# The last gathered tile's value rows are summed on VectorE, and VectorE makes all splits of the dense products

## The chip, the cores and the metric

The kernel runs on one core of one Trainium2 chip. The metric is the device time of one execution in microseconds: before the change the median of three runs is 3572.51 us (3567.39 to 3578.01).

## The reference

One encoder layer on 1024 tokens of width 1024, in float32. The change lies in its last part, PEER, a choice of single-neuron experts. Per block of 128 tokens:

```python
s = einsum('thpd,hpkd->thpk', (xb @ w_q)..., sub_keys)      # 8 heads, 2 halves, 128 keys
idx, best_s = 16 best of the sums of the two halves' 16 best  # per head: 128 experts a token
gate = softmax(best_s)
h = gelu(einsum('thkd,td->thk', u_table[idx], xb), approximate=False)
return einsum('thk,thkd->td', gate * h, v_table[idx])
```

The tables u and v have 16384 rows of 1024 numbers. The result is added to alpha times the block's input, and a LayerNorm gives the output.

## The kernel before

The tokens are eight tiles of 128. The front (projections, attention, the recurrent branch, merge, first LayerNorm) is not touched; each tile's input of PEER is left in HBM as x1d. PEER is done in two ways.

**Gathered tiles** (GATHERED = 0, 1, 2, 6, 7). For each of a tile's 128 choices GpSimd gathers 128 rows of u (one a token) into a place of a ring, 128x1024 float32 or 0.524 MB (experts_in, line 1461), and VectorE multiplies the place with the tile and sums along it (line 1467). After Gelu and the gate the 128x128 coefficients go to HBM. Later the class Rows reads them, turns them with TensorE, gathers rows of v (line 1763) and lets TensorE sum them: a step takes two places, and issues four matmuls, in the profile 8 records named pg, with the coefficients in a sliding window (win). A tile has 64 steps; its sums go through HBM (yd) and finals adds them to alpha times x1d, normalizes and stores, tile after tile.

**Dense tiles** (DENSE = 3, 4, 5). All 16384 experts are evaluated, and the selection is a sparse coefficient matrix. A loop over j = 0 to 127 takes 128 columns of U and rows of V each turn: hidden(j+1, m) makes 24 matmuls of 384 columns into the one PSUM buffer b; csplit(j+1) applies Gelu on ScalarE and multiplies with the selections on VectorE (line 1648), which frees b; values(j, m) makes 18 matmuls of 512 columns (v). Every float32 operand is split in two float32r halves, high by a ScalarE copy (line 291) and low by a subtraction (line 292). usplit and vsplit make four such splits of 128x512 a turn: of U the first on VectorE and the second on GpSimd (UPOOL = (0, 1)), of V every second one on GpSimd (VPAT). The coefficients' split cl is VectorE's. U and V columns come on SP's queue, two and three buffers deep; the coefficients of j >= 44 are reloaded from HBM four at a time.

**The order** is fixed when the program is made. Two background queues put their work between the matmuls: each mm call gives them credit by an estimated duration (columns / 2400 us; line 274 is in mm), times a rate. g.B holds top-k and experts_in of all gathered tiles, whose step k costs 1.46; g.V holds the value steps of Rows, 3 each, two by two in the loop. In the loop the rates are RATEB[1] = 0.46 and RATEV[1] = 0.52, and RATEV[2] = 1.25 once the last gathered tile's u part is done. Each turn also advances finals twice. Instructions of one engine run in this order; GpSimd's queue holds the gathers of both streams and the splits.

After the loop finals adds the dense sums in PSUM to alpha times x1d, normalizes the three tiles and stores them.

Of the kernel before, what the change touches and what calls it, by code (L numbers as in the profile page):

```python
# [10 lines left out]
F32 = mybir.dt.float32  # L11
# [4 lines left out]
AF = mybir.ActivationFunctionType  # L16
OP = mybir.AluOpType
# [9 lines left out]
TKI = 1  # L27
RATEP = (1, 1, 0.9)

RATEB = (2.1, 0.46)  # L30
RATEV = (4.2, 0.52, 1.25)
SEL = (1, 2, 3)
DENSE = (3, 4, 5)
GATHERED = (0, 1, 2, 6, 7)
LATE = (4, 5, 6)

RING = 7
# [3 lines left out]
VCOST = 3.0  # L41
XAT = 14
AENG = "XY"
UPOOL = (0, 1)
VPAT = (0, 2, 4, 6)
VBUF = 3
UBUF = 2
LOMOD = 8
# [13 lines left out]
ALPHA = 2.0 ** 0.25  # L62
# [210 lines left out]
def mm(g, o, l, r, start, stop_):  # L273
    g.pe.matmul(o, l, r, start=start, stop=stop_)  # L274
    n = 1
    for d in r.shape[1:]:
        n *= d
    us = max(n, 256) / 2400.0 if r.dtype == F32R else max(4 * n, 256) / 2400.0
    g.V.tick(us)
    if not g.V.busy:  # L280
        g.B.tick(us)


def mm3(g, o, lh, ll, rh, rl, start, stop_):
    mm(g, o, lh, rh, start, False)
    mm(g, o, lh, rl, False, False)
    mm(g, o, ll, rh, False, stop_)


def split(g, hi, lo, src, lo_eng=None):  # L290
    g.act.copy(hi, src)  # L291
    (lo_eng or g.dve).tensor_sub(lo, src, hi.bitcast(F32))  # L292


class Weights:
# [58 lines left out]
    def ahead(self, most=1):  # L354
        while self.ns <= min(self.n + most * (self.n > 3), self.first - 1):
            self._split()
        while self.ns == self.first and self.nl < len(self.order) and self.nl <= self.n + most:
            self._fetch()
# [21 lines left out]
def run(gen):  # L380
    for _ in gen:
        pass
# [19 lines left out]
def body(ctx, g):  # L402
# [101 lines left out]
    g.spare, g.over = True, False  # L504
    g.rows = Rows(g, GATHERED)
    g.rows.places.add([g.vx.tile([128, D], F32, name=f"vr{i}") for i in range(RING)])
# [754 lines left out]
def layer_norm(g, mt, z):  # L1261

    dve, act = g.dve, g.act
    st = mt.tile([128, 2, 6], F32, name="st", bufs=3)
    for i in range(2):
        dve.bn_stats(st[:, i, :], z[:, i * 512:(i + 1) * 512])
    yield
    mv = mt.tile([128, 2], F32, name="mv", bufs=3)
    dve.bn_aggr(mv, st)
    rs = mt.tile([128, 1], F32, name="rs", bufs=3)  # L1270
    act.activation(rs, mv[:, 1:2], AF.Sqrt, bias=g.eps[:, 1:2])
    yield
    dve.reciprocal(rs, rs)
    yield

    def scale(z, gb):
        dve.scalar_tensor_tensor(z, z, mv[:, 0:1], gb[0], op0=OP.subtract, op1=OP.mult)  # L1277
        dve.scalar_tensor_tensor(z, z, rs, gb[1], op0=OP.mult, op1=OP.add)  # L1278

    yield scale  # L1280
# [166 lines left out]
def experts_in(g, tile_):  # L1447

    dve, act, pool, sp, A, P = g.dve, g.act, g.pool, g.sp, g.A, g.gp
    idx = P.tile([128, 128], I32, name="eidx", bufs=1)  # L1450
    sp.dma_start(idx, g.seld[tile_])
    xt = P.tile([128, D], F32, name="ext")
    sp.dma_start(xt, g.x1d[tile_])
    hh = P.tile([128, 128], F32, name="hh", bufs=1)
    keys, n = g.keys, 0
    yield 1.0
    yield 1.0
    for k in range(128):
        while n < 128 and len(keys.free) > 1:
            keys.alive[n] = place = keys.take()  # L1460
            pool.indirect_dma_start(out=place, out_offset=None, in_=A["u"], in_offset=bass.IndirectOffsetOnAxis(ap=idx[:, n:n + 1], axis=0))  # L1461
            n += 1
        if k == 0:
            yield 1.0
            yield 1.0
        gg = keys.alive.pop(k)
        dve.tensor_tensor_reduce(out=gg, in0=gg, in1=xt, scale=1.0, scalar=0.0, op0=OP.mult, op1=OP.add, accum_out=hh[:, k:k + 1])  # L1467
        keys.give(gg)
        yield 1.46
    if "hh" in g.dbg:  # L1470
        sp.dma_start(g.dbg["hh"][tile_ * 128:(tile_ + 1) * 128, :], hh)
    gate = idx.bitcast(F32)
    sp.dma_start(gate, g.gated[tile_])
    act.activation(hh, hh, AF.Gelu)
    dve.tensor_mul(hh, hh, gate)
    act.dma_start(g.cijd[tile_][:, 0, :], hh)
    yield 0.1


def parts(C, i, a, b):  # L1480

    return [C[:, i, j:j + 8, :].rearrange("p j t -> p (j t)") for j in range(a, b - 7, 8)]


def dense_block(g, C):


    tc, nc, A, ident = g.tc, g.nc, g.A, g.ident
    dve, act, pool, sp, pe = g.dve, g.act, g.pool, g.sp, g.pe
    tiles = DENSE  # L1490
    nt = len(tiles)
    n = nt * 128
# [53 lines left out]

    g.B.rate, g.V.rate = RATEB[0], RATEV[0]
    zx = ExitStack()
# [6 lines left out]
    with tc.tile_pool(name="bp", bufs=BLEAD + 1) as bp, tc.tile_pool(name="cj", bufs=2) as cj:  # L1555
        ab, pb = {}, {}
        for k in range(-BLEAD - 4, n4 + 1):
# [23 lines left out]
            if k > 0:  # L1581
                e = k - 1
                i, o = 4 * e // BLK, 4 * e % BLK
# [7 lines left out]
        run(xt)  # L1591
    g.B.rate, g.V.rate = RATEB[1], RATEV[1]
    u_hl, v_hl, c_hl, phs = {}, {}, {}, {}
    po = [[g.psV.tile([128, 512], F32, name=f"v{i}{m}") for m in range(2)] for i in range(nt)]
# [30 lines left out]
    def usplit(q):  # L1625
        if q < 256:
            u_hl[q] = [lp.tile([128, 512], F32R, name=f"u{x}") for x in "hl"]
            o = q % 2 * 512
            split(g, *u_hl[q], us[q // 2][:, o:o + 512], pool if UPOOL[q % 2] else dve)
            if o:  # L1630
                uload(q // 2 + UBUF)

    def vsplit(q):
        if q < 256:
            v_hl[q] = [lp.tile([128, 512], F32R, name=f"v{x}") for x in "hl"]
            o = q % 2 * 512
            split(g, *v_hl[q], raws[q // 2][:, o:o + 512], pool if q % 8 in VPAT else dve)
            if o:
                load(q // 2 + VBUF)
# [25 lines left out]

    def values(j, m):
        ch, cl = c_hl[j]
        vh, vl = v_hl.pop(2 * j + m)
        for i in range(nt):
            s = slice(i * 128, (i + 1) * 128)  # L1670
            mm3(g, po[i][m], ch[:, s], cl[:, s], vh, vl, j == 0, j == 127)
        if m:
            c_hl.pop(j)

# [12 lines left out]
    fin, old = iter(()), [p for j in range(LOOP, HALF - 7, 8) for i in range(nt) for p in parts(C, i, j, j + 8)]  # L1687
    g.rows.pairs = True
    for j in range(128):
        hidden(j + 1, 0)  # L1690
        usplit(2 * j + 4)
        hidden(j + 1, 1)
        usplit(2 * j + 5)
        csplit(j + 1)
        values(j, 0)
        vsplit(2 * j + 2)
        next(fin, None)
        values(j, 1)
        vsplit(2 * j + 3)
        next(fin, None)  # L1700
        if f"g{GATHERED[-1]}" in g.B.done:
            g.V.rate = RATEV[2]
        if j == 126:

            act.activation(cT[:, 0, 0:1], g.eps[:, 1:2], AF.Sqrt)

        k = (j + 1 - LOOP) // 8 * nt
        if (j + 1) % 8 == 0 and 0 < k <= len(old):
            (g.keys if k == nt else g.rows.places).add(old[k - nt:min(k, len(old) - 4)])
        if j == HALF:  # L1710
            fin = finals(g, tiles, po, old[-4:] + old[0:nt])
    assert f"v{GATHERED[-1]}" in g.V.done
    g.over = True
    run(fin)
    lx.close()
# [101 lines left out]
def finals(g, tiles, po, places):  # L1817


    A, dve, act, sp = g.A, g.dve, g.act, g.sp  # L1820
    gb = places[0:2]
    for m in range(2):
        sp.dma_start(gb[m], A["ln"][2 + m:3 + m, :].to_broadcast([128, D]))
    zd = places[4:7]

    def add(z, y):
        for m in range(2):
            zm = z[:, m * 512:(m + 1) * 512]
            dve.scalar_tensor_tensor(zm, zm, ALPHA, y[m], op0=OP.mult, op1=OP.add)

    z, y = places[2:4]
    for t in GATHERED:
        sp.dma_start(z, g.x1d[t])
        if t == GATHERED[-1]:
            while f"g{t}" not in g.B.done:
                yield
            for t_, z_ in zip(tiles, zd):
                sp.dma_start(z_, g.x1d[t_])
        while f"v{t}" not in g.V.done:
            yield  # L1840
        for _ in range(2):
            yield
        sp.dma_start(y, g.yd[t])
        for _ in range(3):
            yield
        add(z, [y[:, 0:512], y[:, 512:1024]])
        yield
        ln = layer_norm(g, g.pp, z)
        for _ in range(3):
            next(ln)  # L1850
            yield
        next(ln)(z, gb)
        yield
        sp.dma_start(A["out"][t * 128:(t + 1) * 128, :], z)
        yield
    while not g.over:
        yield
    lns = []
    for i, z in enumerate(zd):
        add(z, po[i])  # L1860
        lns.append(layer_norm(g, g.pp, z))
    for _ in range(3):
        for ln in lns:
            next(ln)
    for t, z, ln in zip(tiles, zd, lns):
        next(ln)(z, gb)
        sp.dma_start(A["out"][t * 128:(t + 1) * 128, :], z)


def _pack_w(w):  # L1870
# [54 lines left out]
```

## Time and profile before

| | us |
|---|---|
| median of 3 runs | 3572.51 |
| the profiled execution | 3567.98 |
| its span | 3566.2 |
| PE busy | 3168.3 |
| VectorE (DVE) busy | 2252.5 |
| GpSimd (POOL) busy | 2051.0 |
| ScalarE (ACT) busy | 1161.9 |

The dense loop fills about 2195 to 3543 us of the span. The profile gives busy time by engine and by stretch, groups of equal instructions with their mean duration, what ended each wait, and the chain of work that ended last. A matmul's record overlaps the next one, so the time of a run of matmuls is taken from start to start or from the chain. DMA share is the mean busy share of the 16 DMA engines; packets in flight together can take it a little over 1.

### The profile page before, as it was taken

Reading aid. Unit: us, or ns where it says so; the run is one execution under the profiler, and the core shown is the slowest. Engines: PE = TensorE matmul, PEld = TensorE weight load, DVE = VectorE, ACT = ScalarE, POOL = GpSimd, SP = SyncE. Lnnn points to the kernel's source line nnn. Section 1 sums busy time; section 2 is a strip of 40 time slices with the busy share of each in tenths; the row PEclk is TensorE's granted clock in tenths of the full one; section 3 lists DMA queues with packets and bytes.
Section 4 is the critical chain, followed back from the end, with each engine's and each line's share of the span. In section 5 each row is a group of like instructions: output and inputs, shape, how many; then the busy total and the mean of one; then the engine's idle time right before and its main releaser. Section 6 shows DMA issues by size and latency. Waiting matters only on the chain. (4 is left out here: it accounts for less than half of the span.)

```text
span 3566.2 us, 55635 instructions
## 1 busy us (share of the span) xinstructions
PE 3168.3 (89%) x20656; PEld 2312.2 (65%) x20656; DVE 2252.5 (63%) x5115; ACT 1161.9 (33%) x2448; POOL 2051.0 (58%) x1682
## 2 busy tenths in 40 slices
PE   7899999999997887889677677999999999999997
PEld 5577777875565665567433323877777777776665
DVE  3244423358887997886589755777666767773324
ACT  3443222323431121101244433334333333333332
POOL 2032115315555565653365566888887788886773
PEclk9999999999998788899778899999999999999998
DMA  8373357878897788999799999999999999999994
GB/s 282 112 255 110 105 190 250 306 272 313 287 348 290 272 302 307 350 358 383 278 392 351 354 361 379 369 353 362 386 398 368 394 394 399 397 396 341 389 390 188
DMA packets 369809, 1134.72 MB, mean 318 GB/s; under 512 B 49792, under 2 KB 88448, under 8 KB 367744
## 3 DMA queue, kind: packets, MB, share of 16 engines
q0 software_dynamic: 184320, 671.17, 49.5%
q1 hardware_dynamic: 168496, 430.82, 33.3%
q10 hardware_dynamic: 16720, 29.17, 2.2%
q8 instruction: 162, 2.65, 0.3%
q14 instruction: 111, 0.91, 0.1%
HBM read 997.25 MB, written 133.76 MB: 317 GB/s over the span
## 5 line engine op out<-in xcount | busy, mean ns | idle before, releaser
L1461 POOL DMA_INDIRECT g<-u,eidx x566 | 688.9, 1217 | 520.6 <-DVE hh L1467 193.9
L1467 DVE CUSTOM_DVE_ANT_0 g<-g,ext 128x1024 f32<-128x1024 f32 x566 | 727.9, 1296 | 84.2 <-DMA g<-u,eidx 78.2
L1763 POOL DMA_INDIRECT vr<-v,ve x434 | 454.9, 1048 | 212.0 <-issue 107.2
L292 POOL TENSOR_TENSOR wl<-wraw,wh 128x1024 fp32r<-128x1024 f32 x63 | 152.9, 2427 | 434.3 <-ACT wh L291 335.2
L274 PE MATMUL pg<-vr,win 128*32 128x512 f32 x1736 | 312.9, 643 | 65.6 <-DMA vr<-v,ve 57.9
L274 PE MATMUL b<-xh,uh 128*128 128x384 f32 x1024 | 349.8, 342 | 14.0 <-DVE C L1648 12.6
L274 PE MATMUL b<-xh,ul 128*128 128x384 f32 x1024 | 351.0, 343 | 6.2 <-POOL ul L292 4.3
L274 PE MATMUL b<-xl,uh 128*128 128x384 f32 x1024 | 348.7, 341 | 0.0
L274 PE MATMUL v<-vl,ch 128*128 128x512 f32 x768 | 305.0, 397 | 11.5 <-POOL vl L292 11.4
L274 PE MATMUL v<-vh,ch 128*128 128x512 f32 x768 | 302.5, 394 | 0.0
L274 PE MATMUL v<-vh,cl 128*128 128x512 f32 x768 | 300.8, 392 | 0.0
L274 PE MATMUL pj<-xh,wh 128*128 128x512 f32 x624 | 286.0, 458 | 13.6 <-ACT xh L291 6.6
L291 ACT CAST uh<-uraw 128x512 fp32r<-128x512 f32 x256 | 158.3, 620 | 362.6 <-PE b L274 254.7
L274 PE MATMUL pj<-xl,wh 128*128 128x512 f32 x624 | 260.0, 417 | 2.7 <-DVE xl L292 2.4
L274 PE MATMUL pj<-xh,wl 128*128 128x512 f32 x624 | 259.0, 415 | 0.2 <-issue 0.2
L1763 POOL DMA_INDIRECT C<-v,ve x206 | 212.0, 1029 | 81.4 <-issue 49.0
L292 DVE TENSOR_TENSOR vl<-vraw,vh 128x512 fp32r<-128x512 f32 x128 | 140.8, 1100 | 173.9 <-ACT vh L291 113.0
L291 ACT CAST vh<-vraw 128x512 fp32r<-128x512 f32 x256 | 158.3, 620 | 244.1 <-PE v L274 183.9
L274 PEld LDWEIGHTS v<-ab 128*128 128x128 f32 x768 | 112.5, 217 | 175.6 <-issue 112.9
L292 POOL TENSOR_TENSOR ul<-uraw,uh 128x512 fp32r<-128x512 f32 x128 | 171.6, 1340 | 89.2 <-ACT uh L291 73.6
L274 PEld LDWEIGHTS b<-xh,uh 128*128 128x128 f32 x1024 | 193.5, 189 | 34.5 <-DVE C L1648 14.8
L274 PEld LDWEIGHTS b<-xh,ul 128*128 128x128 f32 x1024 | 193.5, 189 | 32.8 <-issue 24.7
(360 smaller groups left out, 6603.9 us busy)
## 6 DMA issues: line engine op xcount, KB each, us to landing
uraw<-ut SPq DMA_DIRECT2D x128, 512.0 KB
vraw<-vt SPq DMA_DIRECT2D x128, 512.0 KB
wraw<-w SPq DMA_DIRECT2D x72, 512.0 KB
wh<-whd SPq DMA_DIRECT2D x72, 512.0 KB
wl<-whd SPq DMA_DIRECT2D x72, 512.0 KB
whd<-wh SPq DMA_DIRECT2D x71, 512.0 KB
whd<-wl SPq DMA_DIRECT2D x71, 512.0 KB
cd<-S SPq DMA_DIRECT2D x12, 1344.0 KB
```

Of the source, the lines that this page charges most:

```text
L274: g.pe.matmul(o, l, r, start=start, stop=stop_)
L291: g.act.copy(hi, src)
L292: (lo_eng or g.dve).tensor_sub(lo, src, hi.bitcast(F32))
L1461: pool.indirect_dma_start(out=place, out_offset=None, in_=A["u"], in_offset=bass.IndirectOffsetOnAxis(ap=idx[:, n:n + 1], axis=0))
L1467: dve.tensor_tensor_reduce(out=gg, in0=gg, in1=xt, scale=1.0, scalar=0.0, op0=OP.mult, op1=OP.add, accum_out=hh[:, k:k + 1])
L1763: g.pool.indirect_dma_start(out=place, out_offset=None, in_=g.A["v"], in_offset=bass.IndirectOffsetOnAxis(ap=self.meta[i][1][:, t:t + 1], ...
```

## The change

Tile 7 leaves Rows and its matmuls. experts_in now, for this tile, gathers its value rows too, in the same ring and behind the u rows (`ahead`, 256 gathers), and VectorE sums them: 128 scalar_tensor_tensor, each coefficient column times the gathered place plus the running sum, which starts as alpha times x1d. finals normalizes that sum in its place, without the trip through HBM. UPOOL and VPAT give all splits of U and V to VectorE, so GpSimd only gathers in the loop. The rates become 0.58 (0.6 once top-k of tile 7 is done) for g.B and 0.45 for g.V; finals takes four steps a turn once the last tile of Rows is done. In the last turn values goes tile by tile through both halves; after the loop each tile's sum and statistics follow one another, and tile 4 is scaled by one ScalarE and two GpSimd instructions.

```diff
-RATEB = (2.1, 0.46)
-RATEV = (4.2, 0.52, 1.25)
+RATEB = (2.1, 0.58, 0.6)
+RATEV = (4.2, 0.45)
-GATHERED = (0, 1, 2, 6, 7)
+GATHERED = (0, 1, 2, 6)
+LAST = 7
-UPOOL = (0, 1)
-VPAT = (0, 2, 4, 6)
+UPOOL = (0, 0)
+VPAT = ()
 def experts_in(g, tile_):
...
+    ends = 256 if tile_ == LAST else 128
+
+    def ahead():
+        nonlocal n
+        while n < ends and len(keys.free) > 1:
+            keys.alive[n] = place = keys.take()
+            pool.indirect_dma_start(out=place, out_offset=None, in_=A["uv"[n // 128]], in_offset=bass.IndirectOffsetOnAxis(ap=idx[:, n % 128:n % 128 + 1], axis=0))
+            n += 1
...
     act.activation(hh, hh, AF.Gelu)
+    if tile_ != LAST:
+        dve.tensor_mul(hh, hh, gate)
+        act.dma_start(g.cijd[tile_][:, 0, :], hh)
+        yield 0.1
+        return
+    while not g.rows.places.room(1):
+        yield 1.0
+    g.last = z = g.rows.places.take()
+    sp.dma_start(z, g.x1d[tile_])
+    ahead()
+    yield 3.0
+    yield 3.0
     dve.tensor_mul(hh, hh, gate)
+    dve.tensor_scalar(z, z, ALPHA, None, op0=OP.mult)
+    for k in range(128):
+        ahead()
+        gg = keys.alive.pop(128 + k)
+        dve.scalar_tensor_tensor(z, gg, hh[:, k:k + 1], z, op0=OP.mult, op1=OP.add)
+        keys.give(gg)
+        yield 1.46
...
     def values(j, m):
         ch, cl = c_hl[j]
-        vh, vl = v_hl.pop(2 * j + m)
+        if j == 127 and m == 0:
+            return
         for i in range(nt):
             s = slice(i * 128, (i + 1) * 128)
-            mm3(g, po[i][m], ch[:, s], cl[:, s], vh, vl, j == 0, j == 127)
+            for q in (m,) if j < 127 else range(2):
+                mm3(g, po[i][q], ch[:, s], cl[:, s], *v_hl[2 * j + q], j == 0, j == 127)
+        v_hl.pop(2 * j + m)
...
-        if f"g{GATHERED[-1]}" in g.B.done:
-            g.V.rate = RATEV[2]
+        if f"v{GATHERED[-1]}" in g.V.done:
+            next(fin, None)
+            next(fin, None)
+        if f"k{LAST}" in g.B.done:
+            g.B.rate = RATEB[2]
...
 def finals(g, tiles, po, places):
...
+    while f"g{LAST}" not in g.B.done:
+        yield
+    for t, z in zip(tiles, zd):
+        sp.dma_start(z, g.x1d[t])
+    ln = layer_norm(g, g.pp, g.last)
+    for _ in range(3):
+        next(ln)
+        yield
+    next(ln)(g.last, gb)
+    sp.dma_start(A["out"][LAST * 128:(LAST + 1) * 128, :], g.last)
     while not g.over:
         yield
     lns = []
     for i, z in enumerate(zd):
         add(z, po[i])
         lns.append(layer_norm(g, g.pp, z))
...
+        next(lns[i])
+        next(lns[i])
+        if i == 1:
+            next(lns[0])
+            next(lns[1])
+            mv, rs = next(lns[1]).__defaults__
+            dve.scalar_tensor_tensor(mv[:, 0:1], mv[:, 0:1], -1.0, rs, op0=OP.mult, op1=OP.mult)
+            act.activation(z, z, AF.Identity, scale=rs, bias=mv[:, 0:1])
+            g.pool.tensor_mul(z, z, gb[0])
+            g.pool.tensor_add(z, z, gb[1])
+            act.dma_start(A["out"][tiles[1] * 128:tiles[1] * 128 + 128, :], z)
+    next(lns[2])
+    for i in (0, 2):
+        next(lns[i])(zd[i], gb)
+        sp.dma_start(A["out"][tiles[i] * 128:(tiles[i] + 1) * 128, :], zd[i])
```

More of the change, by code (lines that the diff above doesn't have):

```diff
@@ L1274, in layer_norm, with scale @@
     yield
-    def scale(z, gb):
+    def scale(z, gb, mv=mv, rs=rs):
         dve.scalar_tensor_tensor(z, z, mv[:, 0:1], gb[0], op0=OP.subtract, op1=OP.mult)
@@ L1457, in experts_in @@
     yield 1.0
+    ends = 256 if tile_ == LAST else 128
[5 more added lines that the diff above has]
+            n += 1
     for k in range(128):
[L1459 to L1462, printed above, removed]
+        ahead()
         if k == 0:
@@ L1471, in experts_in @@
         sp.dma_start(g.dbg["hh"][tile_ * 128:(tile_ + 1) * 128, :], hh)
-    gate = idx.bitcast(F32)
+    gate = g.tk.tile([128, 128], F32, name="t1") if tile_ == LAST else idx.bitcast(F32)
     sp.dma_start(gate, g.gated[tile_])
     act.activation(hh, hh, AF.Gelu)
-    dve.tensor_mul(hh, hh, gate)
-    act.dma_start(g.cijd[tile_][:, 0, :], hh)
-    yield 0.1
+    if tile_ != LAST:
[10 more added lines that the diff above has]
+    yield 3.0
+    dve.tensor_mul(hh, hh, gate)
+    dve.tensor_scalar(z, z, ALPHA, None, op0=OP.mult)
+    for k in range(128):
+        ahead()
+        gg = keys.alive.pop(128 + k)
+        dve.scalar_tensor_tensor(z, gg, hh[:, k:k + 1], z, op0=OP.mult, op1=OP.add)
+        keys.give(gg)
+        yield 1.46
 def parts(C, i, a, b):
@@ L1711, in dense_block @@
             fin = finals(g, tiles, po, old[-4:] + old[0:nt])
-    assert f"v{GATHERED[-1]}" in g.V.done
+    assert f"v{GATHERED[-1]}" in g.V.done and f"g{LAST}" in g.B.done
     g.over = True
@@ L1833, in finals @@
         sp.dma_start(z, g.x1d[t])
[L1834 to L1838, printed above, removed]
         while f"v{t}" not in g.V.done:
@@ L1861, in finals @@
         lns.append(layer_norm(g, g.pp, z))
[L1862 to L1867, printed above, removed]
+        next(lns[i])
[13 more added lines that the diff above has]
+        sp.dma_start(A["out"][tiles[i] * 128:(tiles[i] + 1) * 128, :], zd[i])
 def _pack_w(w):
```

## The prediction

> **What bounds the kernel now.** I read the summary first (a 3566.2 us span; the profiled execution took 3567.98 us, 4.5 us below the median of 3572.51), then the busy times by stretch, because the change touches only the dense loop and what follows it. The loop over the 128 column groups j fills 2195 to 3543 us. In these rows the columns are the stretch, its length, then busy us of PE, PEld, DVE, ACT and POOL, the granted TensorE clock, the DMA share and GB/s.
>
> ```profile
> 2193.00:2260.00 67.00, 56.66 (x283) 43.43 (x284) 38.28 (x77) 22.63 (x46) 44.68 (x37) 0.92 0.91 342
> 2260.00:2440.00 180.00, 179.71 (x964) 144.07 (x964) 132.64 (x260) 68.81 (x139) 150.20 (x122) 1.00 0.97 367
> 2440.00:3225.00 785.00, 763.52 (x4093) 608.04 (x4092) 544.87 (x719) 290.87 (x587) 660.78 (x547) 0.99 1.01 389
> 2600.00:2650.00 50.00, 50.00 (x269) 40.84 (x268) 33.45 (x47) 18.99 (x38) 43.16 (x37) 1.00 1.02 409
> 2900.00:3200.00 300.00, 295.87 (x1590) 235.68 (x1589) 216.09 (x267) 109.34 (x223) 260.21 (x214) 1.00 1.03 397
> 3225.00:3490.00 265.00, 255.65 (x1426) 176.61 (x1425) 80.09 (x108) 88.27 (x203) 185.46 (x173) 0.98 0.99 374
> 3490.00:3546.00 56.00, 53.68 (x291) 41.97 (x289) 18.20 (x28) 19.13 (x36) 20.95 (x19) 1.00 0.46 167
> ```
>
> Two resources are nearly full at once. PE is busy 96 to 100% of the three long stretches, and the DMA engines stand at a share of 1.01 with 389 GB/s over 785 us; of the two stretches inside that one, the 50 us reach 409 and the 300 us 397. Nothing else is as close: DVE holds 69% of the 785 us and POOL 84%. So work taken from PE counts only as far as the transfers can follow.
>
> The chain of waits shows one turn of the loop on PE (start, us, what):
>
> ```profile
> 2850.43 4.12 PE v L274 x18
> 2854.55 4.24 PE b L274 x24
> 2858.78 0.91 PE v L274 x4
> 2859.69 1.85 PE pg L274 x16
> 2861.55 3.44 PE v L274 x14
> ```
>
> A bare turn is 4.24 + 4.12 = 8.36 us. A pair of value steps (16 pg records, four gathered tiles) costs 1.85 us, and splits a run of v, which then takes 0.91 + 3.44 = 4.35 instead of 4.12: 2.08 us a pair. How many pairs the loop holds is in the groups of its stretch; the next rows give the split instructions there.
>
> ```profile
> L274 PE MATMUL pg<-vr,win 128*32 128x512 f32 x1108 | 171.0, 602 | 2.6 <-DMA vr<-v,ve 2.6
> L274 PE MATMUL pg<-C,win 128*32 128x512 f32 x556 | 98.7, 614 | 7.2 <-DMA C<-v,ve 7.2
> L292 POOL TENSOR_TENSOR vl<-vraw,vh 128x512 fp32r<-128x512 f32 x128 | 177.7, 1388 | 25.7 <-ACT vh L291 24.1
> L292 POOL TENSOR_TENSOR ul<-uraw,uh 128x512 fp32r<-128x512 f32 x128 | 171.6, 1340 | 89.2 <-ACT uh L291 73.6 <-issue 13.8
> L292 DVE TENSOR_TENSOR vl<-vraw,vh 128x512 fp32r<-128x512 f32 x128 | 140.8, 1100 | 173.9 <-ACT vh L291 113.0 <-issue 46.6 <-DMA uraw<-ut 10.1
> L292 DVE TENSOR_TENSOR cl<-C,ch 128x384 fp32r<-128x384 f32 x128 | 130.2, 1017 | 90.5 <-ACT ch L291 75.7 <-issue 9.8 <-ACT vh L291 4.1
> L292 DVE TENSOR_TENSOR ul<-uraw,uh 128x512 fp32r<-128x512 f32 x128 | 108.4, 847 | 131.1 <-ACT uh L291 89.8 <-issue 21.7 <-PE b L274 15.4
> L1467 DVE CUSTOM_DVE_ANT_0 g<-g,ext 128x1024 f32<-128x1024 f32 x156 | 222.8, 1435 | 0.0
> ```
>
> 1664 pg records at 8 a step are 208 steps, 104 pairs. The loop's transfers, summed over the five window rows that do not overlap, are 503 MB.
>
> **Part 1: tile 7 leaves PE.** Its 64 steps, 32 pairs, go: 32 x 2.08 = 66.6 us of PE work. PE's floor for the loop falls from 128 x 8.36 + 104 x 2.08 = 1286 to 1070 + 72 x 2.08 = 1220 us. In place of them stand 128 scalar_tensor_tensor of 128x1024 on DVE (Part 2), behind the reductions of tile 7 in the same queue. Tile 7's 128 value gathers remain, now into the ring of u rows; with them remain their bytes. What vanishes from the DMA is small: the sums are no longer written to and read from HBM (2 x 0.52 MB) and two small tables (0.26 MB): 1.3 MB of 503.
>
> **Part 2: the splits go to DVE.** A split on DVE is long now because POOL does one at the same time. The timeline has it both ways (start, us): beside a POOL subtraction 1.66 us, without one 0.69 us; the product C, with an input in PSUM, and cl take 0.56 us.
>
> ```profile
> 3490.21 1.29 POOL L292 TENSOR_TENSOR vl<-vraw,vh 128x512 fp32r<-128x512 f32 x1
> ...
> 3490.40 1.66 DVE L292 TENSOR_TENSOR vl<-vraw,vh 128x512 fp32r<-128x512 f32 x1 [4.30 <-issue]
> 3493.92 0.69 DVE L292 TENSOR_TENSOR ul<-uraw,uh 128x512 fp32r<-128x512 f32 x1 [1.86 <-PE b L274]
> 3496.85 0.56 DVE L1648 TENSOR_TENSOR C<-b,C 128x384 f32<-128x384 f32 x1 [2.25 <-ACT b L1647]
> 3497.99 0.56 DVE L292 TENSOR_TENSOR cl<-C,ch 128x384 fp32r<-128x384 f32 x1 [0.58 <-ACT ch L291]
> ```
>
> POOL's 349 us of subtractions go. DVE takes 512 splits at 0.69 = 353 us instead of 249, and its cl shrinks from 130 to 128 x 0.56 = 72 us: 46 us more in all. The chain's last instruction is the operation of the value sums, with two SBUF inputs and nothing on POOL beside it:
>
> ```profile
> 3560.93 1.28 DVE C L1278
> ```
>
> 128 of them are 164 us. DVE's 814 us in the loop become about 1000, less some 25 that 156 and more reductions no longer wait for POOL (1435 ns now), over 1310: 75%. In one turn late in the loop, with the planner's 0.6 x 7.68 / 1.46 = 3.16 rows: 3.16 x 1.28 + 4 x 0.69 + 2 x 0.56 = 7.9 us of 10.2. That fits; the wait behind a row that has not landed is the second rival. While top-k of tile 7 runs, DVE holds 132.64 of 180 us; two more splits, less waiting and a planner 0.58 / 0.46 times as quick make that some 84%. I charge 0.25 us a turn there.
>
> **Part 3: what the planner sends to the DMA.** Its credit a turn is 24 x 0.16 + 18 x 0.2133 = 7.68. Now a turn brings 7.68 x 0.46 / 1.46 = 2.42 u rows and 2 x 7.68 x 0.52 / 3 = 2.66 v rows: 5.08 gathers of 0.524 MB, plus 1.05 MB of U and V columns and, from j = 44, 0.2 MB of selections. After, it is 3.16 + 2.30 = 5.46 gathers once top-k 7 is done: 2.86 + 1.05 + 0.2 = 4.11 MB, which needs 10.3 us at 400 GB/s, while PE needs only 8.36 + 0.576 x 2.08 = 9.56. So **the DMA ends last** there. In the sum:
> - the first 67 us stay (23 MB);
> - while top-k 7 runs, to about j = 24, a turn brings some 4.6 gathers, 3.46 MB, and PE with DVE's charge sets 9.8 us: 18 turns, 176 us, 62 MB;
> - both streams end near j = 122 (72 pairs at 0.576 a turn, two steps ahead), so the last 56 us look like the last row above (9 MB);
> - the other 408 MB run at the DMA's rate: 1049 us at 389, 997 us at 409. I take 400, a little over the best 300 us, whose PE still set part of the pace: 1019 us.
>
> Together 67 + 176 + 56 + 1019 = 1318 against 1353 for the same rows: 35 us less, bounds 5 and 57.
>
> The Trainium skill ("DMA: Bandwidth & Descriptors", section Measured) states 425 GB/s for a 16 MB load by one core alone, near its fabric ceiling of 435. No stretch here exceeds 409; by the page's figure the 408 MB would take 960 us, and PE would end last instead, which is the first rival's case.
>
> **Part 4: the tail.** Now DVE normalizes tile 7 when the last matmuls run, and only then adds the dense sums:
>
> ```profile
> 3540.15 0.69 DVE vl L292
> 3540.85 1.20 DVE C L1829 x2
> ...
> 3546.52 3.59 DVE C L1829 x6
> 3550.11 3.57 DVE st L1266 x6
> ```
>
> Tile 7 is to be finished earlier, and the last turn sums tile by tile, so the first add can start near 3541.7. Adds 3.59, statistics 3.57, some 1.2 of small ones and four scalings instead of six (5.0) end at 3555, where the last scaling quoted in Part 2 ends at 3562.2: 7 us earlier. Against that, tile 4's scaling goes to ACT and two POOL operations, and POOL needs 2.4 us for 128x1024:
>
> ```profile
> L292 POOL TENSOR_TENSOR wl<-wraw,wh 128x1024 fp32r<-128x1024 f32 x63 | 152.9, 2427 | 434.3 <-ACT wh L291 335.2 <-PE s L274 42.7 <-PE po L274 26.4
> ```
>
> By the pair of rows in Part 2, DVE's scalings, with two SBUF inputs, stand still meanwhile: up to 4.9 us back. Bounds 2 to 7; I take 4.
>
> **Sum.** 3567.98 - 35 - 4 = 3529, and with the 4.5 us between this execution and the median, **3534 us**.
>
> **The rivals.** *PE alone sets the loop.* For it: PE was 97% busy in 2440:3225 and turned at its own pace with 389 GB/s; the waits for POOL's splits would go too (11.4 us, in the rows of the next rival). Against it: 4.11 MB in 9.56 us is 430 GB/s. Time: 66.6 + 7 less, 3498 us. 15%.
>
> *DVE's queue becomes the bound, and the kernel slower.* All splits and the product C, which frees the one PSUM buffer of the hidden sums, now stand on DVE behind 3.16 rows a turn that may not have landed. The waits of PE and, below, what a long one does:
>
> ```profile
> PE b L274 <- DVE C L1648: 12.6, 4, 6.3
> PE v L274 <- POOL vl L292: 11.4, 19, 2.2
> ```
>
> ```profile
> 2214.49 0.69 PE L274 MATMUL b<-xh,uh 128*128 128x384 f32 x1 [5.04 <-DVE C L1648]
> 2214.98 0.52 PE L274 MATMUL b<-xl,uh 128*128 128x384 f32 x1
> 2215.30 0.52 PE L274 MATMUL b<-xh,ul 128*128 128x384 f32 x1
> ```
>
> After 5.04 us idle the matmuls step by 0.32 us, where the 24 in 4.24 us above step by 0.177. One such wait costs some 6.5 us (5.04, and about ten matmuls at 0.15 more). The Trainium skill ("TensorE: Matmul & The Clock Gate", section What's actually happening) puts the half rate behind an idle window of about 3.4 us: these rows agree. While PE waits the transfers go on, so a few cost nothing; past the 39 us of the forecast, six, a net loss begins, and eight make it measurable. At one every seventh of the 98 late turns, 14 waits, it is 91 - 39 = 52 us slower: 3625. Against it: DVE at 77% and seven rows ahead in the ring. 12%.
>
> *It does not do all it says.* Tile 6's last normalization takes some 12 steps of the finals, four a turn from j = 122; with the load of the dense inputs it may slip past j = 127 into the tail (6 to 12 us), and if the DMA holds only 389 the loop gains 5. Time: 3572.5 - 5 - 4 + 9 = 3572. 13%.
>
> **How the numbers follow.** The forecast has 60%. A measurement of this kernel tells about 0.3%, 11 us, from no change. Forecast and first rival are faster (75%), and a little of the third; the rest of it is mostly same. Faster 0.77, same 0.11, slower 0.12. The forecast's own bounds are 3572.5 - 57 - 7 = 3508 and 3572.5 - 5 - 2 = 3566; taking in the times of the first rival and the third, the range is 3498 to 3572.
>
> **What would show it.** DVE's u and v splits at 0.69 us and cl at 0.56; no POOL subtraction in the loop; 1152 pg records in the loop instead of 1664; 395 to 405 GB/s from j = 24 to 120; turns of about 10.2 us, with PE idle some 8% and waiting for rows or for splits held up behind rows; 18 to 21 us from the last matmul to the end. I am wrong if the DMA passes 410 GB/s and turns take 9.6 us, or if PE's waits for DVE come with the DMA below 380.

## The result, and the profile after

| | before | after |
|---|---|---|
| median | 3570.3 us (4 runs, 3567.39 to 3578.01) | 3524.66 us (4 runs, 3510.81 to 3530.58) |
| ratio to before | | 0.9852, 95% interval 0.9822 to 0.9883 |
| profiled execution | 3567.98 us | 3530.58 us |
| first to last matmul of the dense loop | 1348.5 us | 1307.0 us |
| last matmul of the loop to the end | 22.8 us | 17.5 us |
| start of the loop | 2195.0 us | 2204.3 us |

The kernel is 45.6 us faster where 38.5 were forecast. Between the two profiled executions the loop gives 41.5 us, the tail 5.3, and the front, which the change does not touch, takes 9.3 back. On the chips of the experiments the loop began anywhere from 2170 to 2207 us, while three profiles of after's loop, one of them with one place fewer in a ring, agree within 0.5 us. So below, the loop's length carries the comparisons of profiles, and the ratio to the kernel before, run on the same chip, those of times.

The stretches after, in the columns of the prediction (last: granted clock, DMA share, GB/s):

```profile
2260.00:2440.00 180.00, 180.00 (x971) 147.43 (x970) 143.86 (x335) 71.64 (x142) 103.41 (x91) 1.00 1.01 390
2440.00:2640.00 200.00, 194.42 (x1039) 157.66 (x1039) 143.80 (x245) 73.24 (x149) 127.23 (x106) 0.99 1.01 396
2640.00:2900.00 260.00, 240.46 (x1257) 196.52 (x1256) 186.09 (x318) 91.53 (x184) 164.17 (x139) 0.97 1.03 402
2900.00:3200.00 300.00, 284.06 (x1485) 230.37 (x1487) 212.57 (x311) 103.54 (x212) 183.46 (x156) 0.97 1.03 399
3200.00:3400.00 200.00, 190.71 (x1011) 155.52 (x1004) 144.45 (x180) 67.30 (x141) 127.05 (x107) 0.98 1.03 401
3450.00:3510.00 60.00, 59.61 (x300) 51.35 (x300) 36.87 (x58) 28.71 (x47) 0.00 (x0) 1.00 0.38 129
```

From 2640 to 3400 us the transfers stand at 399 to 402 GB/s, and PE, which was busy for 97% of 2440:3225 before, is idle for 5 to 8% of these stretches. POOL has fallen to 61% of 2900:3200 from 87%. The groups show what VectorE pays and what PE still does for gathered tiles:

```profile
L1474 DVE CUSTOM_DVE_ANT_0 g<-g,ext 128x1024 f32<-128x1024 f32 x160 | 194.9, 1218 | 6.2 <-DMA g<-u,eidx 6.1
...
L293 DVE TENSOR_TENSOR ul<-uraw,uh 128x512 fp32r<-128x512 f32 x256 | 176.0, 691 | 209.0 <-ACT uh L292 173.0 <-issue 17.4 <-PE pg L275 8.0
L293 DVE TENSOR_TENSOR vl<-vraw,vh 128x512 fp32r<-128x512 f32 x256 | 175.7, 689 | 43.1 <-ACT vh L292 29.6 <-issue 12.9
...
L275 PE MATMUL pg<-vr,win 128*32 128x512 f32 x824 | 128.0, 611 | 3.1 <-DMA vr<-v,ve 2.9 <-issue 0.2
...
L1499 DVE SCALAR_TENSOR_TENSOR C<-g,hh,C 128x1024 f32<-128x1024 f32 x80 | 102.3, 1279 | 0.0
...
L293 DVE TENSOR_TENSOR cl<-C,ch 128x384 fp32r<-128x384 f32 x128 | 71.5, 559 | 80.3 <-ACT ch L292 68.0 <-issue 11.7 <-ACT vh L292 0.6
```

512 splits now take 352 us where 256 took 249; each is the 0.69 us of a split with no subtraction on POOL beside it. Nearly all of PE's waits now end with VectorE, and behind ScalarE's u casts stands a transfer:

```profile
PE b L275 <- DVE C L1672: 52.3, 18, 8.2
PE v L275 <- DVE vl L293: 6.9, 3, 3.4
```

```profile
2738.41 20.93 DMA uraw<-ut
...
2759.43 0.63 ACT uh L292
...
2761.91 0.60 DVE ul L293
2762.52 0.48 DVE C L1672
...
2763.04 5.41 PE b L275 x22
```

In the chain of waits a 512 KB load of U columns needs 21 us; cast, split and C follow, and PE starts b late. Whether this wait costs anything is asked below. The tail:

```profile
3508.04 0.75 PE v L275 x2
...
3508.82 0.69 DVE C L1859
3509.50 1.21 DVE st L1267 x2
...
3517.41 1.63 DVE C L1278
...
3519.07 3.24 DVE C L1279
```

VectorE adds the first tile while PE still sums the others. Two of the last scalings take 1.63 and 3.24 us instead of 1.2 and 1.28: GpSimd scales tile 4 at that time.

### The profile page after: what moved, and what is told of

It is laid out like the page before. It is cut to its first block, busy times and chain, and to the rows that moved or that the text cites. A ratio compares the mean times of both kernels' runs of the same rounds, so it can differ in the third digit from the quotient of the medians.

```text
span 3528.8 us, 54819 instructions
## 1 busy us (share of the span) xinstructions
PE 3112.8 (88%) x20141; PEld 2317.7 (66%) x20141; DVE 2374.5 (67%) x5495; ACT 1146.9 (33%) x2383; POOL 1750.4 (50%) x1428
## 4 chain that ended last, share of the span: by engine, by line
PE 48%; DVE 18%; DMA 14%; issue 10%; POOL 4%; ACT 2%; another core or an unknown queue 0%; SPq 0%; ACTq 0%; POOLq 0%; DVEq 0%
PE b L275 12%; PE v L275 10%; PE pj L275 7%; DMA uraw<-ut 7%; PE s L275 5%; DVE g L1474 4%; PE o L275 4%; PE pg L275 3%; DMA g<-u,eidx 3%; POOL g L1465 2%; PE S L275 2%; DMA vr<-v,ve 2%; DVE ab L1562 1%; PE a L275 1%; DMA s<-scd 1%
## 5 line engine op out<-in xcount | busy, mean ns | idle before, releaser
L1474 DVE CUSTOM_DVE_ANT_0 g<-g,ext 128x1024 f32<-128x1024 f32 x569 | 699.8, 1238 | 80.0 <-DMA g<-u,eidx 70.5
L1793 POOL DMA_INDIRECT vr<-v,ve x359 | 403.8, 1125 | 252.3 <-issue 84.8
L275 PE MATMUL pg<-vr,win 128*32 128x512 f32 x1436 | 263.0, 650 | 66.7 <-DMA vr<-v,ve 63.3
L293 DVE TENSOR_TENSOR ul<-uraw,uh 128x512 fp32r<-128x512 f32 x256 | 176.0, 691 | 209.0 <-ACT uh L292 173.0
L1793 POOL DMA_INDIRECT C<-v,ve x153 | 169.8, 1110 | 83.7 <-issue 37.5
L275 PEld LDWEIGHTS b<-xl,uh 128*128 128x128 f32 x1024 | 197.5, 193 | 16.6 <-issue 12.4
L293 DVE TENSOR_TENSOR vl<-vraw,vh 128x512 fp32r<-128x512 f32 x256 | 175.7, 689 | 43.1 <-ACT vh L292 29.6
```

The source lines that it names most:

```text
L1793: g.pool.indirect_dma_start(out=place, out_offset=None, in_=g.A["v"], in_offset=bass.IndirectOffsetOnAxis(ap=self.meta[i][1][:, t:t + 1], ...
```

## The experiments

My theory was that the bytes of the transfers set the pace after the change. The rivals were that VectorE's queue does, or the latency of single loads.

**One part alone: the splits.** On the kernel before:

```diff
-UPOOL = (0, 1)
+UPOOL = (0, 0)
-VPAT = (0, 2, 4, 6)
+VPAT = ()
```

> The kernel before, with all splits of U and V on VectorE and nothing else changed. My theory (transfers bind the dense loop after the change, and PE and transfers are nearly level before it): the splits alone remove PE's waits for GpSimd's subtractions (11.4 + 4.3 us) and a few slow matmuls behind them, 5 to 15 us: 3555 to 3565. Rival (the subtractions on GpSimd, which hold up VectorE, are the main cost that the change removes): 30 us or more, 3540 or less.

Measured: 3528.68 us against 3544.05 of before on that chip, ratio 0.9955 (0.9935 to 0.9974), some 16 us; the loop 1329.2 us, 19 less than before's. That is a little over my figures and far from the rival's. PE is busy for 1117 of the 1140 us from 2260 to 3400. The splits alone give less than half of the gain.

**One part alone: the sums.** On the kernel after, the two lines set back to (0, 1) and (0, 2, 4, 6).

> The kernel after, with half of the U and V splits back on GpSimd. My theory: VectorE gets longer (its two-input operations wait beside a subtraction, about 1 us each), but the transfers set the pace, so most of the gain stays: 5 to 25 us above the kernel after, 3530 to 3550. Rival (VectorE's queue is as near the limit as the transfers): 35 us or more above it, 3560 or more.

Measured: 3577.12 us, ratio 1.0081 (1.0052 to 1.0109); the loop is 1382.8 us, 76 longer than after's and 34 longer than before's. My figure fell, and the rival's came, though whether by its cause was open: taking 32 pairs from PE makes the kernel *slower* as long as GpSimd keeps its splits. The parts are not additive. PE waits here for GpSimd:

```profile
PE b L275 <- POOL ul L293: 62.7, 35, 4.9
PE v L275 <- POOL vl L293: 31.4, 40, 5.7
```

What became scarce was not clear yet: VectorE, whose operations lengthen beside GpSimd's subtractions, or GpSimd itself. The last four experiments return to it.

**Fewer bytes, same work.**

```diff
         while n < ends and len(keys.free) > 1:
+            if n >= 128 and n % 2:
+                n += 1
+                continue
...
-        gg = keys.alive.pop(128 + k)
+        gg = keys.alive[128 + k - k % 2]
```

(and the place is given back after its second sum).

> The kernel after, which gathers only every second of tile 7's value rows and sums each place twice; VectorE does the same 128 sums, 64 gathers or 33.6 MB are left out, and tile 7's result is therefore another. My theory (bytes set the pace): 33.6 MB at 400 GB/s are 84 us of transfers, from about j = 80 on; turns there fall from about 10.2 to PE's 9.56 us: 25 to 40 us less than after, 3485 to 3500. Rival (VectorE's queue or PE sets the pace): within 8 us of after.

Measured: 3466.4 us, ratio 0.9779 (0.9754 to 0.9805); the loop 1281.3 us, 26 less. From j = 80 to 120 a turn took 9.56 us instead of 10.31, which is the 9.56 us that the prediction gave PE alone. In the late stretches PE is busy for 96 and 100%, and the transfers fall below 400 GB/s:

```profile
2900.00:3200.00 300.00, 289.17 (x1540) 237.01 (x1539) 221.85 (x309) 108.21 (x221) 149.88 (x131) 0.98 0.99 368
3200.00:3400.00 200.00, 200.00 (x1077) 164.25 (x1077) 155.34 (x192) 73.49 (x149) 80.36 (x69) 1.00 0.89 322
```

VectorE's share of 3200:3400 rose from 72 to 78% and did not hold anything up: the gathers (their bytes, or the GpSimd time that goes with them) set the pace there, and VectorE's queue does not.

**VectorE relieved.** The other side of the same question:

```diff
-        dve.scalar_tensor_tensor(z, gg, hh[:, k:k + 1], z, op0=OP.mult, op1=OP.add)
+        dve.scalar_tensor_tensor(z[:, 0:512], gg[:, 0:512], hh[:, k:k + 1], z[:, 0:512], op0=OP.mult, op1=OP.add)
```

> The kernel after, with VectorE's 128 value sums over the first 512 of the 1024 columns only; all rows are still gathered, and half of tile 7's expert output is left out. VectorE has about 128 x 0.6 = 75 us less. My theory (bytes set the pace): within 8 us of after. Rival (VectorE's queue sets the pace in the late turns): 20 us or more below after.

Measured: 3524.22 us, ratio 0.9854 (0.981 to 0.9898), loop 1302.7 us. The kernel after itself, run beside it, took 3529.99 us:

> The kernel after, unchanged, on the chip of the next three kernels, so that they can be set against it. Both theories: 0.982 to 0.988 of the kernel before.

Ratio 0.9867 (0.9821 to 0.9912), loop 1306.5 us. A sum took 0.746 us instead of 1.279, so VectorE had 68 us less to do, and the loop gave some 4 us: VectorE is not the bound in the turns that hold the sums.

**The late loads of U columns.**

```diff
-RING = 7
+RING = 6
-UBUF = 2
+UBUF = 3
```

> The kernel after, with three buffers for the columns of U instead of two, and one place fewer for the value rows that TensorE sums. In the profile after, PE's longest waits begin with a load of U columns that lands 21 us after its issue. My theory (bytes set the pace): PE waits elsewhere, within 10 us of after, 3515 to 3535. Rival (the latency of these loads, with two buffers too few, is what costs): 25 us or more below after, 3500 or less.

Measured: 3498.8 us, ratio 0.9881 (0.9855 to 0.9907); that chip's kernel before took 3544.05, so the low time is the chip's. The loop is 1303.8 us, 3 less than after's. PE's waits for C fall from 52 to 25 us, and no wait of ScalarE for uraw is left among its longest; in exchange VectorE and PE wait for gathered rows:

```profile
PE b L275 <- DVE C L1672: 25.0, 12, 4.6
PE v L275 <- DVE vl L293: 8.1, 7, 2.7
PE pg L275 <- DMA vr<-v,ve: 7.6, 7, 1.6
PE pg L275 <- DMA C<-v,ve: 3.9, 4, 1.5
```

```profile
DVE g L1474 <- DMA g<-u,eidx: 43.7, 18, 5.6
DVE C L1474 <- DMA C<-u,eidx: 24.9, 7, 5.9
```

PE's longest wait was worth 3 us: a buffer changes who waits while the bytes arrive at 399 GB/s as before.

**A later end.**

```diff
-RATEB = (2.1, 0.58, 0.6)
-RATEV = (4.2, 0.45)
+RATEB = (2.1, 0.57, 0.585)
+RATEV = (4.2, 0.44)
...
-            next(fin, None)
-            next(fin, None)
+            for _ in range(8):
+                next(fin, None)
```

> The kernel after, with the planner's rates lowered by 2 to 3% (0.57, 0.585 and 0.44 for 0.58, 0.6 and 0.45) and the finals quicker once the last tile of Rows is done, so that both gather streams end some three turns later and the last turns carry more of the bytes. My theory (bytes set the pace from about j = 24 on, and in the last 60 us the transfers are at 0.38): about 2.5% fewer bytes a turn, 8 to 18 us below after. Rival (the pace is set by waits, not by bytes): within 5 us of after or, where the finals slip into the tail, above.

Measured: 3529.53 us, ratio 0.9857 (0.9821 to 0.9892), loop 1305.4 us: no gain, which is the rival's figure and not mine. But the turns did get shorter, as fewer bytes a turn should make them: from j = 24 to 120 the mean fell from 10.32 us (the unchanged kernel on the same chip) to 10.13, some 18 us in all. The end took them back: from j = 122 to the last matmul it is 76 us instead of 57. The last pair of tile 6 comes two turns later, and with ten steps of the finals a turn, tile 6's addition and statistics fall among VectorE's last splits:

```profile
3470.64 3.64 DMA yd<-vr
...
3474.33 3.59 DMA C<-yd
3477.95 1.29 DVE C L1859 x2
3479.24 1.21 DVE st L1267 x2
...
3481.12 1.29 DVE ul L293 x2
3482.42 0.48 DVE C L1672
...
3483.03 6.60 PE b L275 x24
```

In this chain of waits tile 6's sums go to HBM and back, VectorE adds them and takes their statistics, and only then splits the U columns for the next b, whose 24 matmuls take 6.60 us instead of 4.24. The idle time of the transfers hardly changed either: the last gathered packet lands in turn 125 instead of 122, and the stretch from there to the last matmul shrinks from 62 to 48 us, but it runs at 141 and 87 GB/s. Set against 400 GB/s, (1 - 141 / 400) x 62 = 40 us of it are idle in the unchanged kernel and (1 - 87 / 400) x 48 = 38 us here.

**The tail.**

```diff
-            mv, rs = next(lns[1]).__defaults__
...
-            act.activation(z, z, AF.Identity, scale=rs, bias=mv[:, 0:1])
-            g.pool.tensor_mul(z, z, gb[0])
-            g.pool.tensor_add(z, z, gb[1])
-            act.dma_start(
+            next(lns[1])(z, gb)
+            sp.dma_start(
```

> The kernel after, with tile 4's last scaling on VectorE too, without the ScalarE and the two GpSimd instructions. In the profile after, two of VectorE's last scalings take 1.63 and 3.24 us beside GpSimd instead of 1.2 to 1.28. My theory (they stand still while GpSimd holds the port): two more scalings (2.5 us) against 2.3 us of standing still, so the same time within 2 us from the last matmul to the end. Rival (GpSimd really takes work off): 2.5 us or more longer.

Measured: 17.4 us from the last matmul to the end, 17.5 with GpSimd's help on the same chip (3524.68 and 3529.99 us). Two more scalings cost what two scalings lost beside GpSimd. So the tail's gain is left to the order of the sums and tile 7's earlier end, which were not run apart.

**What is scarce when GpSimd keeps work.** Two kernels put work on GpSimd that nobody waits for, twice a turn, with all splits on VectorE:

```diff
-RING = 7
+RING = 6
+    scr = g.pp.tile([128, 512], F32, name="scr")
...
             split(g, *u_hl[q], us[q // 2][:, o:o + 512], pool if UPOOL[q % 2] else dve)
+            if q % 2:
+                pool.tensor_sub(scr, scr, scr)
```

(the same beside each second split of V). In the question that follows, 8 to 9 ms/1000 are 0.8 to 0.9%.

> The kernel after, with two subtractions of 128x512 a turn on GpSimd that nobody waits for (a scratch tile in place, at the places where half of the splits stood; one place fewer for value rows makes the room). Why did the sums without the move of the splits cost 8 to 9 ms/1000 more than the kernel before, with PE waiting 63 and 31 us for GpSimd's splits? Theory L (the lock: VectorE's two-input operations stand still beside GpSimd's subtractions, and its queue has no room for that with the sums in it): two-input operations of VectorE lengthen by up to 2 x 1.3 us a turn, and the loop gets 30 us or more longer than after's 1307, though no split is on GpSimd. Theory Q (the queue: PE waits because the splits on GpSimd stand behind gathers that wait for places): within 12 us of after, since PE waits for nothing on GpSimd here.

Measured: 3578.13 us, ratio 0.9996 (0.9974 to 1.0017), loop 1353.2 us, 46 longer. By itself that speaks for theory L. The other kernel has memsets instead: two of 128x512 and one of 128x128 each time.

> The same with memsets in place of the subtractions, as long in sum (about 1.2 us, twice a turn) but reading nothing. Theory L, with the lock on GpSimd's reads: VectorE's operations keep 0.69 and 0.56 us, loop within 10 us of after. Theory Q: also within 12 us of after. If the loop is 30 us longer here too, then it is GpSimd's time itself, through late gathers, that costs.

Measured: 3624.79 us, ratio 1.0125 (1.0101 to 1.015), loop 1405.2 us, 98 longer, although VectorE is untouched. VectorE beside the subtractions and beside the memsets:

```profile
L293 DVE TENSOR_TENSOR ul<-uraw,uh 128x512 fp32r<-128x512 f32 x248 | 217.8, 885 | 63.0 <-ACT uh L292 56.2 <-ACT win L1826 2.9 <-PE b L275 2.3
```

```profile
L293 DVE TENSOR_TENSOR ul<-uraw,uh 128x512 fp32r<-128x512 f32 x238 | 162.9, 689 | 117.6 <-ACT uh L292 101.5 <-issue 10.2 <-PE b L275 4.7
```

885 ns and 689 ns: VectorE's splits lengthen beside the subtractions only, and the kernel in which they don't is the slower one. That is neither theory L nor theory Q but the third reading, GpSimd's time itself. Its timeline beside the memsets, and in the kernel after:

```profile
3002.51 1.49 POOL L1803 DMA_INDIRECT vr<-v,ve  x1 [0.30 <-issue]
3004.30 1.02 POOL L1465 DMA_INDIRECT g<-u,eidx  x1 [0.30 <-issue]
3005.32 0.54 POOL L1657 MEMSET scr<- 128x512 f32 x1
3005.92 0.53 POOL L1658 MEMSET scr<- 128x512 f32 x1
3006.50 0.21 POOL L1659 MEMSET scr<- 128x128 f32 x1
3007.23 0.98 POOL L1465 DMA_INDIRECT g<-u,eidx  x1 [0.52 <-issue]
```

```profile
3004.72 0.94 POOL L1793 DMA_INDIRECT vr<-v,ve  x1 [0.30 <-issue]
3007.01 0.93 POOL L1465 DMA_INDIRECT C<-u,eidx  x1 [1.35 <-DMA g<-u,eidx]
3009.54 1.31 POOL L1465 DMA_INDIRECT C<-v,eidx  x1 [1.60 <-DMA g<-u,eidx]
3012.11 0.93 POOL L1465 DMA_INDIRECT g<-v,eidx  x1 [1.25 <-DVE ul L293]
```

In front of most gathers stand 0.30 us that count as idle and are not free: they stand there in the kernels without room too (the first three lines above). With them, GpSimd beside the memsets is full; in the kernel after it waits for places. Over 2260 to 3400 us, with the gaps over 0.7 us as the time that GpSimd really has to spare:

| kernel | POOL busy | gaps over 0.7 us | GB/s | loop, us |
|---|---|---|---|---|
| before | 931 | 57 | 382 | 1348.5 |
| after | 705 | 266 | 398 | 1307.0 |
| sums only | 976 | 18 | 376 | 1382.8 |
| with subtractions | 965 | 25 | 382 | 1353.2 |
| with three memsets | 899 | 16 | 367 | 1405.2 |

Two controls settle it: the place fewer, and a third of the memsets' instructions.

> The kernel after, with one place fewer for the value rows that TensorE sums: what the two kernels with scratch work on GpSimd also had. Theory G (they were longer because GpSimd's own queue was full: between 2260 and 3400 us it has some 266 us of gaps over 0.7 us in the kernel after, and 16 to 25 us in them): within 8 us of after's loop of 1307 us. Rival R (the missing place is what cost): 1325 us or more.

> The same, with one memset of 128x512 twice a turn instead of three. Theory G: about 2 x (0.53 + 0.1) us a turn, 140 us over the 112 turns or so in 2260 to 3400 us, out of the 266 us that GpSimd has to spare; the loop stays within 12 us of the kernel with one place fewer. Rival W (a memset disturbs the gathers or the transfers, however full GpSimd is): a third or more of the 98 us that three memsets cost, 1340 us or more.

Measured: 3499.72 us, ratio 0.9887 (0.9855 to 0.9919), loop 1306.5 us for the place fewer; 3509.32 us, ratio 0.9921 (0.989 to 0.9951), loop 1303.5 us with one memset twice a turn. GpSimd then has 175 us of gaps over 0.7 us left, and the loop is not longer; with three memsets it has 16, and the loop is 98 us longer. Theory G holds: work on GpSimd was free until its queue was full, and from then on the gathers came later and the loop grew. This also settles what the halved rows left open: 118 us more of GpSimd's time cost nothing, so what leaving out gathers saved was their transfers and not GpSimd's time. Here is the stretch 2260 to 3400 us in the kernel after, with one memset and with three:

```profile
2260.00:3400.00 1140.00, 1089.65 (x5754) 887.50 (x5753) 830.76 (x1387) 407.24 (x827) 705.32 (x596) 0.98 1.03 398
```

```profile
2260.00:3400.00 1140.00, 1091.83 (x5742) 892.24 (x5741) 830.45 (x1361) 404.96 (x825) 822.84 (x821) 0.98 1.02 397
```

```profile
2260.00:3400.00 1140.00, 1049.91 (x5346) 834.53 (x5346) 773.16 (x1316) 383.21 (x769) 898.62 (x1163) 0.97 0.98 367
```

How much of the 46 us beside the subtractions is VectorE's lengthening and how much the full queue was not separated, since that kernel had both; the same goes for the 76 us of the sums alone. None of the variants that compute the whole result beats the kernel after beyond the intervals: the best ratio, 0.983 (0.9789 to 0.9872) for the tail on VectorE, has after's 0.9867 inside its interval.

## Why the prediction was right, and where it was not

**Part 1** held: PE's value records fell to 824 + 344 = 1168 by the stretch's rows, 1152 in the loop itself, where 1152 were forecast.

**Part 2** held in its prices (0.69, 0.56 and 1.28 us measured as 0.69, 0.56 and 1.279), and VectorE is no bound: relieved of 68 us, the loop gave 4. The 0.25 us a turn that I charged for VectorE while top-k runs did not show either: PE was busy for all of 2260:2440, and a turn took 9.47 us where 9.8 were forecast. But the step "nothing else is as close" was wrong. POOL's 84% of busy time leaves out the issue time between gathers; by its gaps GpSimd had only 57 of 1140 us to spare before. So I priced the move of the splits as a charge on VectorE with less waiting as its return, and missed its main worth: it makes the room without which the quicker u and v stream of Part 3 cannot be issued. The sums without it were slower by 0.8%. That the forecast came out all the same was luck in this part: the change has both parts, but no term of the sum stood for this room.

**Part 3** held, with 400 GB/s measured as 399 to 402 from 2640 us on and a mean turn of 10.32 us from j = 24 to 120 where 10.2 were forecast. The loop shrank by 41.5 us against my 35 (5 to 57). Cut at turns 6, 24 and 122, it took 70, 171, 1010 and 57 us; the terms of the sum were 67, 176, 1019 and 56, for rows that are 4.5 us longer than the loop. Removing bytes with their gathers gave 26 us, while more buffers or less VectorE work gave 3 to 4. Whether the 400 GB/s are the limit of the DMA engines or of the gathers in flight was not run, beyond one place fewer for value rows, which cost nothing. What I read loosely is the evidence of before: I called the DMA nearly full by its share of 1.01, but a share of 0.98 stood beside 367 GB/s with GpSimd full. The share near 1 doesn't tell a full DMA from a slowly fed one; the GB/s that no variant passes over a long stretch says more.

The Trainium skill's 425 GB/s ("DMA: Bandwidth & Descriptors", section Measured) is for one large load; these 4 KB rows and short reloads stay at 397 to 399 GB/s over 2260 to 3400 us, and at 396 to 403 in its stretches of 200 us and more from 2640 us on, in every variant of the kernel after whose GpSimd has time left and whose bytes were not cut. So the first rival, which needed 430, fell.

**Part 4**: the tail gave 5.3 us, of bounds 2 to 7, and 4 were taken; its 17.5 us lie half a microsecond under the 18 to 21 that were to show it. The charge for GpSimd's part was right in kind (2.4 us of standing still, of at most 4.9), and that part is worth nothing.

**The second rival's** mechanism is there in part. PE waits 52 us for C, 18 times, but in the chain behind late U columns (ScalarE waited 17 times for such, 112.9 us) and not, as I had it, behind gathered rows; and it has next to no price: with 25 us instead the loop is 3 us shorter. While PE waits, the transfers go on. Neither it nor the slip of the finals into the tail came about.

## What to carry to other kernels

Count an engine that issues gathers by the time it really has left, issue gaps included, and not by its busy share: filler work on it was free here until the queue was full, and then delayed the gathers behind it. Where transfers set the pace, the longest wait in the profile may be only the place where the lateness shows; ask what moves the bytes sooner or removes them before adding a buffer. Two parts of a change can be a loss and a small gain alone and a larger gain together.

## What the runs showed of the hardware

- A memset on GpSimd (0.53 us for 128x512) leaves VectorE's splits, which have two inputs in SBUF, at 689 ns; subtractions (1.12 and 1.19 us on average) lengthen U's splits to 885 ns on average. The Trainium skill ("SBUF — State Buffer", section Who interferes with whom) says that such operations contend only with GpSimd instructions that read SBUF: both runs agree.
- The DMA share stays at 0.98 to 1.03 while the rate goes from 367 GB/s (beside three memsets) to 402 (the kernel after, 2640 to 2900 us).
- Most gathers have 0.30 us in front of them in which GpSimd counts as idle: a GpSimd with 899 us of busy time in 1140 had no room left.
- The time up to the dense loop differs by up to 37 us from chip to chip and run to run (2170.1 to 2207.1 us), while three profiles of after's loop agree within 0.5 us.
